# Moving three waits of a split-precision decoder trunk: gate statistics, the first convolution, and the first head's scores, transposes and values

## The chip, the cores and the metric

The kernel runs on one core of a Trainium2 chip. The metric is device time of one execution in microseconds (us), the median of the runs shown; all arithmetic is in the kernel, and the weights come from HBM in every execution. The engines are called as the profile calls them: PE is TensorE (PEld its weight loads), DVE is VectorE, ACT is ScalarE, POOL is GpSimd and SP is SyncE, which here issues the DMAs.

## The reference

A decoder trunk of two layers over 256 tokens with 1024 channels, in float32. Layer 0 mixes tokens by a gated short convolution, layer 1 by dilated window attention with 8 heads of 128 and three groups per head, each group with its own q, k, v and its own dilation. After each mixer come a squared-ReLU MLP (1024 to 4096 and back) and a gated per-layer input. In short:

```python
def rmsnorm(x, g):
    y = xf * lax.rsqrt(jnp.mean(xf * xf, axis=-1, keepdims=True) + RMS_EPS)
    return y * g
...
h = h + mixed
h = h + squared_relu_mlp(rmsnorm(h, norm_mlp[i]), mlp_w_up[i], mlp_w_down[i])
ple_gate = jax.nn.sigmoid(rmsnorm(h, norm_ple[i]) @ ple_w_gate[i])
h = h + ple_gate * (p[i] @ ple_w_proj[i])
```

Attention of a head: for each of the three groups scores of q and k under that group's mask, softmax, and the groups joined by their log-sum-exp. The kernel does this as one softmax over the 512 masked scores of the three groups, which is the same.

## The kernel before, in words

**Split products.** Every float32 matrix product is made of three products of rounded parts. A weight slab of up to 8 blocks of 128x128 is loaded by SP (L321), ACT rounds it to a high part `whi` (L331) and DVE subtracts to get the low part `wlo` (L280, in `sub`). There are 6 buffers for split slabs, and a slab is asked for up to 5 slabs ahead (L337). Activations are split likewise into pairs (`split_into`, L402 on ACT and L280 on DVE; `h_ready`, L411 on ACT and L412 on DVE). A block (L342) is 3 matmuls of kind "n" or "t", or 2 of kind "w", all at L363.

**The plan.** `make_plan` writes the order of the work as one list: blocks, and between them steps ("do", name, ...). `tile_trunk` emits the instructions in that order, and the build then sets a fixed order of instructions on each engine, which may differ a little from the list: an instruction whose operands its own estimate has ready later can come behind some that follow it in the list. At run time each engine takes its instructions strictly in its order.

**The convolution (layer 0).** For each pair of channel tiles c come the products C, X and B. `stat(0)` (L441) makes the norm's statistics: matmuls with ones (L445), a power on POOL (L435), two small corrections on DVE, and a diagonal matrix of the result, split in two parts (L477, L478). `spread(0)` (L480) multiplies the diagonals with ones on PE (L486), and ACT copies the row out of PSUM (L488). `conv(0)` (L548) needs that row; it has one memset of 0.1 us on POOL (L551). Both stand behind block k = 1 of C of the second pair.

**The gate of layer 0 (`gate_plan`).** Four products `gate(j)` of 16 blocks each, j being a pair of channel tiles. `gate_out(j)` (L590) multiplies by the spread row on DVE (L592), takes the sigmoid on ACT (L593), multiplies and adds on DVE (L594, L600) and makes by `h_ready` the pair x3_j that layer 1 multiplies, and the sums of squares for its norm. The first product of attention, head 0's q and k, takes x3_0 to x3_3 in order, three groups side by side.

**Attention.** Head 0's q and k of all three groups (kind "n") come first, with `stat(3)` and `spread(3)`, which scales the tables `cosr` and `sinr` of the rotation (L491, L492) on DVE. Then for each group `qk_out` (L604) rotates q and k on POOL: one multiply by cosr (L606), two by sinr (L609) and an add (L615). Group 0 is then split (L402 on ACT, L280 on DVE). A later head h runs 16 blocks of q and k per group (kind "w"), `add_up` (L382 on ACT, L383 on DVE) and `qk_out` after each group, then v (16 blocks, "t", `v_out`). The head before is worked off in between: `scores(h-1)` (L632; matmuls of group 0 at L638, of groups 1 and 2 at L641; mask and maximum on DVE at L644; exponential and scaling on ACT at L648 and L650) behind group 0 of head h, `turn(h-1)` (L653, eight transposes at L659) behind group 2, and `values(h-1)` (L667; L674, L680, out of PSUM at L691 and L692) behind block k = 5 of v. None of the three issues a DMA or a POOL instruction. PSUM has 8 banks from one pool; each accumulator or score tile takes one. Plain activation tiles (`act`) have 13 buffers, pairs 20.

Of the kernel before, what the change touches and what calls it, by code (L numbers as in the profile page):

```python
# [18 lines left out]
NK = D // P  # L19
# [46 lines left out]
def mlp_plan(layer):  # L66
    up, down, x = f"up{layer}", f"down{layer}", f"x{3 * layer + 1}"
    plan = head_start(up, "u", x, ("up_out",))
    for j in range(2, FF // P // 2):
        for k in range(NK):  # L70
            for i in (0, 1):
                plan.append(("w", up, k, 2 * j + i, ("u", j), i, x))
        plan.append(("do", "up_out", j))
        if j == 3:
            plan.append(("do", "stat_rows", 3 * layer + 1))
        if (layer, j) == (0, 8):
            plan.append(("do", "rope"))
    for j in range(NP):
        for k in range(FF // P):
            for i in (0, 1):  # L80
                plan.append(("n" if j == NP - 1 else "w", down, k, 2 * j + i, ("d", j), i, "u"))
        plan.append(("do", "down_out", layer, j))
    return plan


def proj_plan():
    plan = []
    for j in range(NP):
        for k in range(PLE // P):
            for i in (0, 1):  # L90
                plan.append(("n", "proj0", k, 2 * j + i, ("p", j), i, "p0"))
        plan.append(("do", "proj_out", j))
    return plan


def gate_plan():
    def gate(j, ks):
        return [("n", "gate0", k, 2 * j + i, ("g", j), i, "x2") for k in ks for i in (0, 1)]

    plan = gate(0, range(6)) + gate(1, range(6)) + gate(0, (6, 7)) + [("do", "stat", 2)]  # L100
    plan += gate(1, (6, 7)) + gate(2, range(5)) + [("do", "spread", 2)]
    plan += [("do", "gate_out", 0), ("do", "gate_out", 1)] + gate(2, range(5, NK)) + [("do", "gate_out", 2)]
    return plan + gate(3, range(NK)) + [("do", "gate_out", 3)]


def last_plan():

    plan = []

    def gate(ks, b, c):  # L110
        return [("t", "gate1", k, c, ("g", b, c), b, "x5") for k in ks]

    for k in range(NK - 3):
        for b in (0, 1):
            plan += gate((k,), b, 0) + gate((k,), b, 1)
        if k == 3:
            plan.append(("do", "stat", 5))
        if k:
            plan.append(("do", "turn_h", k - 1))
    for b in (0, 1):  # L120
        for c in (0, 1):
            plan += gate(range(NK - 3, NK), b, c)
            plan.append(("do", "last_gate", b, c))
            if b and c:
                plan.append(("do", "last_scale", 0, 0))
            cuts = 2 if b and c else 1
            for m in range(cuts):
                for k in range(PLE // P):
                    plan.append(("t", "proj1", k, c, ("p", b, c, m), b, "p1", m, cuts))
                plan.append(("do", "last_out", b, c, m, cuts))  # L130
        plan.append(("do", "last_rms", b))
    return plan + [("do", "last_scale", 1, 0), ("do", "last_scale", 1, 1)]


def make_plan():
    plan = [("do", "begin")]
    plan += proj_plan()
    for c in range(NP):
        for s, what in ((1, "C"), (2, "X"), (0, "B")):
            for k in range(NK):  # L140
                for i in (0, 1):
                    kind = "w" if what == "X" else "n"
                    plan.append((kind, "sc_in", k, s * NK + 2 * c + i, (what, c), i, "x0"))
                if c == 0 and (what, k) in ((("C", 3), ("C", 7), ("X", 1), ("X", 3))):
                    plan.append(("do", "squares", 0, (3, 7, 1, 3).index(k) if what == "C" else 2 + (k == 3)))
                if (c, what, k) == (0, "B", 2):
                    plan.append(("do", "stat", 0))
                if (c, what, k) == (1, "C", 1):
                    plan += [("do", "spread", 0), ("do", "conv", 0)]
            if what == "X":  # L150
                plan.append(("do", "add_up", (what, c)))
        if c:
            plan.append(("do", "conv", c))

    def mix(key, j, ks):
        return [("n", key, k, 2 * j + i, ("o", j), i, "y") for k in ks for i in (0, 1)]

    for k in range(6):
        plan += mix("sc_out", 0, (k,)) + mix("sc_out", 1, (k,))
    for j in range(NP):  # L160
        plan += mix("sc_out", j, range(6 if j < 2 else 0, NK)) + [("do", "mix_out", 0, j)]
    plan += mlp_plan(0) + gate_plan()

    plan.append(("do", "masks"))

    def qk(h, g, ks):
        return [
            ("w" if h else "n", "qkv", k, (i, g, h), ("qk", h, g), i, "x3") for k in ks for i in (0, 1)
        ]

    def v(h, ks):
        return [("t", "v", k, h, ("v", b, h), b, "x3") for k in ks for b in (0, 1)]

    for kp in range(NP):
        if kp == NP - 1:
            plan.append(("do", "stat", 3))
        for g in range(GROUPS):
            plan += qk(0, g, (2 * kp, 2 * kp + 1))
    plan += [("do", "add_up", ("qk", 0, g)) for g in range(GROUPS)]
    plan += v(0, (0, 1)) + [("do", "spread", 3)]  # L180
    plan += [("do", "qk_out", 0, g) for g in range(GROUPS)] + v(0, range(2, NK)) + [("do", "v_out", 0)]

    def sums(h, g):
        return [("do", "add_up", ("qk", h, g)), ("do", "qk_out", h, g)]

    for h in range(1, HEADS):
        plan += qk(h, 0, range(NK)) + sums(h, 0) + [("do", "scores", h - 1)]
        plan += qk(h, 1, range(NK)) + sums(h, 1)
        plan += qk(h, 2, range(NK)) + [("do", "turn", h - 1)] + sums(h, 2)
        plan += v(h, range(6)) + [("do", "values", h - 1)] + v(h, range(6, NK)) + [("do", "v_out", h)]  # L190

    last = HEADS - 1
    plan += [x for k in (0, 1, 2) for j in range(NP) for x in mix("w_o", j, (k,))]
    plan.append(("do", "scores", last))
    plan += [x for k in (3, 4) for j in range(NP) for x in mix("w_o", j, (k,))]
    plan.append(("do", "turn", last))
    plan += [x for k in (5, 6) for j in range(NP) for x in mix("w_o", j, (k,))]
    plan.append(("do", "values", last))
    for j in range(NP):
        plan += mix("w_o", j, (7,)) + [("do", "mix_out", 1, j)]  # L200
    plan += mlp_plan(1) + [("do", "last_load")] + last_plan()
    return plan
# [658 lines left out]
```

## Time and profile before

| | us |
|---|---|
| median of 3 runs (lowest, highest) | 806.48 (806.38, 806.66) |
| the profiled execution, its own time | 803.92 |
| its span, from the first to the last instruction | 802.1 |
| PE busy in that span | 779.4 |
| DVE, ACT, POOL busy | 584.2, 443.1, 180.9 |

The profile is of one execution. Times in its rows are counted from the start of the span. Busy time of PE counts a matmul from its start to its modelled end, so neighbouring matmuls overlap. An idle time is put down to the event that ended it.

### The profile page before, as it was taken

To read this page: it belongs to the slowest core of one execution; us is meant where nothing else is said; L and a number is where in the kernel's file an instruction comes from. 1 tells how busy PE (TensorE), PEld (TensorE's weight loads), DVE (VectorE), ACT (ScalarE), POOL (GpSimd) and SP (SyncE) were. 2 spreads that over 40 slices of the span, in tenths; PEclk is the share of its full clock that TensorE was granted. 3 is DMA by queue.
4 is the path that set the end of the run, shared out by engine and by line. 5 is a ranking of instruction groups with operands and counts; after the bars stand their busy time and mean duration, and the time that the engine had idled before them with its cause. 6 is when DMAs were issued, how large, how long until landed. Compare 5 with 4: busy or idle time off the path is not lost.

```text
span 802.1 us, 12773 instructions
## 1 busy us (share of the span) xinstructions
PE 779.4 (97%) x4986; PEld 713.9 (89%) x4986; DVE 584.2 (73%) x818; ACT 443.1 (55%) x672; POOL 180.9 (23%) x117
## 2 busy tenths in 40 slices
PE   8999999999999999959999999999999999999996
PEld 8999998888888999949999899999988888888985
DVE  6987778898456658857697798788599787555555
ACT  8655565666444446636556656647566565444453
POOL 0100000000000000197487687687000000000001
PEclk9999999999999999979999999999999999999998
DMA  8865555555555554534464465465546555565521
GB/s 288 291 211 190 181 187 177 192 179 189 184 186 187 183 185 154 171 93 142 125 204 148 145 194 154 149 186 172 178 152 201 189 186 190 188 198 185 185 79 54
DMA packets 41676, 140.98 MB, mean 176 GB/s; under 512 B 4752, under 2 KB 5136, under 8 KB 41616
## 3 DMA queue, kind: packets, MB, share of 16 engines
q1 hardware_dynamic: 41616, 140.17, 54.8%
q8 instruction: 39, 0.64, 0.3%
q14 instruction: 21, 0.17, 0.1%
HBM read 139.10 MB, written 1.05 MB: 175 GB/s over the span
## 4 chain that ended last, share of the span: by engine, by line
PE 91%; DVE 3%; POOL 3%; issue 1%; ACT 1%; DMA 1%; SPq 0%; POOLq 0%; DVEq 0%; ACTq 0%
PE acc_d L363 22%; PE acc_u L363 22%; PE acc_qk L363 15%; PE acc_v L363 7%; PE acc_o L363 6%; PE acc_g L363 5%; PE acc_X L363 3%; PE acc_B L363 2%; PE acc_C L363 2%; POOL rot L609 1%; DVE wlo L280 1%; PE sc L641 1%; PE o L680 1%; PE tp L659 1%; PE o L674 1%
## 5 line engine op out<-in xcount | busy, mean ns | idle before, releaser
L280 DVE TENSOR_TENSOR wlo<-raw,whi 128x1024 fp32r<-128x1024 f32 (+3 forms) x273 | 367.2, 1353 | 133.5 <-ACT whi L331 132.8
L331 ACT ACTIVATE whi<-raw 128x1024 fp32r<-128x1024 f32 (+3 forms) x273 | 276.9, 1017 | 198.2 <-PE acc_d L363 87.3
L363 PE MATMUL acc_d<-u,whi 128*128 128x512 f32 (+1 forms) x640 | 180.6, 350 | 0.0
L363 PE MATMUL acc_u<-x,whi 128*128 128x512 f32 x512 | 179.4, 395 | 0.0
L363 PE MATMUL acc_d<-u,wlo 128*128 128x256 f32 x512 | 143.9, 281 | 0.0
L363 PE MATMUL acc_u<-x,wlo 128*128 128x256 f32 x512 | 143.4, 280 | 0.0
L363 PE MATMUL acc_qk<-x,whi 128*128 128x512 f32 (+1 forms) x432 | 135.6, 371 | 1.9 <-DVE x L412 1.9
L363 PEld LDWEIGHTS acc_d<-u,whi 128*128 128x128 f32 x640 | 111.9, 189 | 16.9
L435 POOL TENSOR_TENSOR n<-v,power 128x4 f32<-128x4 f32 (+1 forms) x6 | 6.5, 1087 | 518.7 <-DVE v L455 515.9
L363 PEld LDWEIGHTS acc_u<-x,whi 128*128 128x128 f32 x512 | 95.9, 187 | 22.4
L363 PE MATMUL acc_qk<-x,wlo 128*128 128x256 f32 x384 | 107.9, 283 | 0.5 <-ACT x L411 0.3
L363 PEld LDWEIGHTS acc_d<-u,wlo 128*128 128x128 f32 x512 | 97.1, 190 | 0.0
L363 PEld LDWEIGHTS acc_u<-x,wlo 128*128 128x128 f32 x512 | 96.7, 189 | 0.0
L363 PEld LDWEIGHTS acc_qk<-x,whi 128*128 128x128 f32 x432 | 78.1, 190 | 16.2 <-DVE x L412 2.5
L609 POOL TENSOR_TENSOR rot<-qk,sinr 16x512 f32<-16x512 f32 x48 | 90.6, 1887 | 3.3
L363 PEld LDWEIGHTS acc_qk<-x,wlo 128*128 128x128 f32 x384 | 72.8, 191 | 0.9 <-ACT x L411 0.9
L363 PE MATMUL acc_v<-whi,x 128*128 128x384 f32 x256 | 68.8, 339 | 0.0
L606 POOL TENSOR_TENSOR qk<-qk,cosr 128x512 f32<-128x512 f32 x24 | 36.9, 1539 | 54.4 <-DVE qk L383 47.7
L363 PEld LDWEIGHTS acc_v<-whi,x 128*128 128x128 f32 x256 | 46.5, 188 | 0.0
L363 PE MATMUL acc_o<-y,whi 128*128 128x256 f32 x256 | 46.0, 283 | 0.0
L615 POOL TENSOR_TENSOR qk<-qk,rot 48x512 f32<-48x512 f32 x24 | 43.9, 1828 | 1.7
L363 PE MATMUL acc_v<-wlo,x 128*128 128x384 f32 x128 | 42.8, 335 | 0.0
(164 smaller groups left out, 1036.3 us busy)
## 6 DMA issues: line engine op xcount, KB each, us to landing
raw<-in_w SPq DMA_DIRECT2D x232, 512.0 KB, 3.6
raw<-in_w SPq DMA_DIRECT2D x32, 384.0 KB, 3.1
raw<-in_w SPq DMA_DIRECT2D x7, 256.0 KB, 4.7
h<-in_xT SPq DMA_DIRECT2D x4, 256.0 KB, 5.0
out<-ht SPq DMA_DIRECT2D x4, 256.0 KB, 2.0
pt<-in_pT SPq DMA_DIRECT2D x2, 256.0 KB, 3.6
mask<-in_mask SPq DMA_DIRECT2D x2, 256.0 KB, 4.3
gain<-in_gain SPq DMA_DIRECT2D x2, 256.0 KB, 4.5
```

Source lines behind the costliest of these rows:

```text
L280: nc.vector.tensor_tensor(out, a, f32(b), ALU.subtract)
L331: nc.scalar.activation(hi[:, :width], t[:, :width], AF.Copy)
L363: nc.tensor.matmul(to, a, b, start=n == 0 and name not in opened, stop=n == len(products) - 1 and left[name, half if kind == "n" else 0] == 0,
L435: nc.gpsimd.tensor_tensor(y, v, power[:, : v.shape[1]], ALU.pow)
L606: nc.gpsimd.tensor_tensor(t, p, both(cosr), ALU.mult)
L609: nc.gpsimd.tensor_tensor(r[dst : dst + 16], p[src : src + 16], sinr[src : src + 16].unsqueeze(1).to_broadcast([16, 2, S]), ALU.mult,)
L615: nc.gpsimd.tensor_tensor(t[:48], t[:48], r[:48], ALU.add)
L641: nc.tensor.matmul(ps[:, (g + 1) * P : (g + 2) * P], t[:, 0, own], t[:, 1, own], start=True, stop=True)
L659: nc.tensor.transpose(ps[n // 2][:, n % 2, b * P : (b + 1) * P], sm[:, n * P : (n + 1) * P], ident)
L674: nc.tensor.matmul(ps[:, 0, :], a, b[:, kb, :], start=kb == 0 and n == 0, stop=False, skip_group_check=True)
L680: nc.tensor.matmul(ps[:, 0, b * P : (b + 1) * P], v12[:, b, g * P : (g + 1) * P], t[:, g, b * P : (b + 1) * P], start=False, stop=g == 1, ...
```

## The change

It touches only the order of the plan. In the gate, `stat(2)` comes behind 16 blocks, `spread(2)` behind 28 and `gate_out(0)` with it; they came behind 28 and 42. The order of the gate's blocks among themselves stays. In the convolution, `spread(0)` and `conv(0)` come behind block k = 4 of C instead of k = 1. In attention, the first head alone is worked off later: `scores(0)` behind group 2 of head 1 instead of group 0, `turn(0)` behind block k = 5 of head 1's v, and `values(0)` behind group 0 of head 2. Later heads keep their order.

```diff
-    plan = gate(0, range(6)) + gate(1, range(6)) + gate(0, (6, 7)) + [("do", "stat", 2)]
-    plan += gate(1, (6, 7)) + gate(2, range(5)) + [("do", "spread", 2)]
-    plan += [("do", "gate_out", 0), ("do", "gate_out", 1)] + gate(2, range(5, NK)) + [("do", "gate_out", 2)]
-    return plan + gate(3, range(NK)) + [("do", "gate_out", 3)]
+    plan = gate(0, range(6)) + gate(1, (0, 1)) + [("do", "stat", 2)] + gate(1, range(2, 6)) + gate(0, (6, 7))
+    plan += [("do", "spread", 2), ("do", "gate_out", 0)] + gate(1, (6, 7)) + [("do", "gate_out", 1)]
+    return plan + [x for j in (2, 3) for x in (*gate(j, range(NK)), ("do", "gate_out", j))]
...
-                if (c, what, k) == (1, "C", 1):
+                if (c, what, k) == (1, "C", 4):
                     plan += [("do", "spread", 0), ("do", "conv", 0)]
...
     for h in range(1, HEADS):
-        plan += qk(h, 0, range(NK)) + sums(h, 0) + [("do", "scores", h - 1)]
-        plan += qk(h, 1, range(NK)) + sums(h, 1)
-        plan += qk(h, 2, range(NK)) + [("do", "turn", h - 1)] + sums(h, 2)
-        plan += v(h, range(6)) + [("do", "values", h - 1)] + v(h, range(6, NK)) + [("do", "v_out", h)]
+
+        late, steps = h == 1, [[("do", what, h - 1)] for what in ("scores", "turn", "values")]
+        plan += qk(h, 0, range(NK)) + ([("do", "values", 0)] if h == 2 else []) + sums(h, 0)
+        plan += [] if late else steps[0]
+        plan += qk(h, 1, range(NK)) + sums(h, 1) + qk(h, 2, range(NK)) + steps[late ^ 1] + sums(h, 2)
+        plan += v(h, range(6)) + steps[2 - late] + v(h, range(6, NK)) + [("do", "v_out", h)]
```

## Rows read from the trace of the kernel before

**Rows 1.** The page, busy time of each engine, share of the span, instructions.

```profile
PE 779.4 (97%) x4986; PEld 713.9 (89%) x4986; DVE 584.2 (73%) x818; ACT 443.1 (55%) x672; POOL 180.9 (23%) x117
```

**Rows 2.** Waits of PE, whole span: us in total, times, longest.

```profile
PE sc L641 <- POOL qk L615: 7.9, 2, 4.8
PE acc_qk L363 <- DVE x L412: 1.9, 3, 0.6
...
PE spread L486 <- DVE diag L477: 0.7, 1, 0.7
```

**Rows 3.** Windows: head 0's q and k, head 1, head 2; length, then busy per engine.

```profile
341.80:383.44 41.64, 32.84 (x183) 29.61 (x183) 25.98 (x31) 19.18 (x33) 35.70 (x23) 0.88 0.41 122
383.44:412.51 29.07, 29.07 (x183) 27.01 (x182) 21.28 (x29) 17.20 (x30) 18.26 (x11) 1.00 0.48 151
...
311.91:333.24 21.33, 19.00 (x151) 17.98 (x150) 18.84 (x39) 12.74 (x20) 1.01 (x1) 1.00 0.56 175
```

**Rows 4.** The chain that ended last, in order of time: start, length, what.

```profile
83.76 23.04 PE acc_o L363 x192
...
360.27 12.37 PE acc_qk L363 x64
...
379.76 0.71 PE o L674 x6
...
381.36 2.08 PE acc_v L363 x12
383.44 5.55 PE acc_qk L363 x32
...
390.60 11.11 PE acc_qk L363 x64
```

**Rows 5.** Timeline of DVE around the gate: start, length, what, idle before.

```profile
305.53 0.68 DVE L592 TENSOR_TENSOR gs<-acc_g,row 128x512 f32<-128x512 f32 x1
...
310.77 0.89 DVE L412 SCALAR_TENSOR_TENSOR x<-hr,gains,x 128x256 fp32r<-128x256 f32 x2 [0.85 <-ACT x L411]
...
328.21 0.87 DVE L412 SCALAR_TENSOR_TENSOR x<-hr,gains,x 128x256 fp32r<-128x256 f32 x2
```

**Rows 6.** Timeline of POOL, rotations of heads 0 and 1.

```profile
338.37 1.34 POOL L606 TENSOR_TENSOR qk<-qk,cosr 128x512 f32<-128x512 f32 x1 [6.48 <-DVE cosr L491]
...
356.67 1.25 POOL L615 TENSOR_TENSOR qk<-qk,rot 48x512 f32<-48x512 f32 x1
...
362.53 1.28 POOL L615 TENSOR_TENSOR qk<-qk,rot 48x512 f32<-48x512 f32 x1
...
382.21 2.16 POOL L615 TENSOR_TENSOR qk<-qk,rot 48x512 f32<-48x512 f32 x1
```

**Rows 7.** Tile qk on POOL: duration ns min/median/max, first and last start.

```profile
L609 POOL TENSOR_TENSOR rot<-qk,sinr x48: 1252/1896/2184, 339.8 to 558.1; 16x512 f32<-16x512 f32 x48
L606 POOL TENSOR_TENSOR qk<-qk,cosr x24: 1267/1297/2191, 338.4 to 553.7; 128x512 f32<-128x512 f32 x24
L615 POOL TENSOR_TENSOR qk<-qk,rot x24: 1252/2154/2285, 345.5 to 560.4; 48x512 f32<-48x512 f32 x24
```

**Rows 8.** Timeline of ACT, splits of group 0 and first softmax.

```profile
346.81 0.63 ACT L402 ACTIVATE qk<-qk 128x512 fp32r<-128x512 f32 x1 [5.78 <-POOL qk L615]
...
361.41 0.72 ACT L648 ACTIVATE sm<-sm,st 128x512 f32<-128x512 f32 x1 [8.29 <-DVE st L647]
...
363.85 0.63 ACT L402 ACTIVATE qk<-qk 128x512 fp32r<-128x512 f32 x1 [1.62 <-POOL qk L615]
...
366.44 0.71 ACT L650 ACTIVATE sm<-sm,st 128x512 f32<-128x512 f32 x1
```

**Rows 9.** The page's group of DVE's weight splits: busy, mean ns, idle before.

```profile
L280 DVE TENSOR_TENSOR wlo<-raw,whi 128x1024 fp32r<-128x1024 f32 (+3 forms) x273 | 367.2, 1353 | 133.5 <-ACT whi L331 132.8
```

**Rows 10.** Windows of 1 us: length, busy PE, PEld, DVE, ACT, POOL, then granted clock.

```profile
352.00:353.00 1.00, 0.00 (x0) 0.00 (x0) 1.00 (x2) 1.00 (x1) 1.00 (x2) 0.83 0.97 266
...
362.00:363.00 1.00, 1.00 (x5) 0.90 (x4) 0.32 (x2) 0.23 (x2) 0.92 (x2) 0.55 0.87 135
```

## The prediction

> **What bounds the kernel now.** I first read the busy times: PE is busy 97% of the span [rows 1], so only two things can be won, a hole in PE or a stretch at a lower clock; every matmul stays. Next I read what PE waited for [rows 2]. Three waits stand there that the change is near: 7.9 us in the first head's scores for POOL's rotation, 1.9 us in head 0's q and k for the gate's x3 pairs, 0.7 us for the diagonal of the convolution's statistics. A wait shows only time in which PE had nothing at all in flight, so I priced each hole by windows instead [rows 3]. Head 1 takes 41.64 us, head 2 takes 29.07, with the same instructions: 12.57 us are lost there, more than the wait says. Part of that is clock: it fell between 352 and 353 us, with PE idle in that window, to the lower level of 1.2 GHz (a mean of 0.83 in that microsecond), and came back only between 362 and 363 (a mean of 0.55) [rows 10], though PE ran on again from 358. So some 4.9 us of work ran at half speed, 2.4 us lost. Head 0's q and k take 21.33 us for 144 matmuls; at 0.12 us each (192 in 23.04 [rows 4]) and 0.37 for the statistics between them they need 17.65, so 3.7 us are lost.
>
> All times below are on the axis of the trace of before; what an earlier part wins shifts the later ones as a whole.
>
> **The gate.** Nothing is added: the order of the weights stays, so no DMA is moved; the only POOL instruction of these steps is one power, with POOL idle around it. A block is 3 x 0.12 = 0.36 us, so the statistics come 12 blocks or 4.3 us earlier and the spread 14 blocks or 5.0 us. gate_out(0) began on DVE at 305.53 [rows 5]; its own accumulators are complete at the new spread, so it can begin at about 300.5. The pair x3_0 was complete at 311.66, x3_3 at 329.08, one each 5.8 us [rows 5]. Shifted by 5.0 and at the same pace they come at 306.6, 312.5, 318.3 and 324.1; PE wants them at 311.9 and then each 12 blocks or 4.3 us later, the last at 324.9. So nothing waits any more, with 0.8 us to spare at the last. The new cover of statistics to spread is 12 blocks, 4.3 us. If DVE puts a split (1.35 us [rows 9]) into that chain, PE waits a little at the spread and the last pair is late by 0.5. Bounds: 3.7 gained, or 1.9 if only the wait shown goes and the rest stays. I take 3.6, as DVE has holes before 310 that the earlier chain fills.
>
> **The convolution.** The spread moves by 3 x 2 x 3 = 18 matmuls or 2.2 us, and the wait was 0.7 [rows 2]: 0.7 gained. conv(0) gives its PSUM banks back up to 1.5 us later; five banks are held then and the next product takes two, so two are left. Bounds: 0.7 gained, or 0.5 lost if the banks were short. I take 0.7.
>
> **The first head.** No instruction is added. Three things decide, in this order.
>
> First, scores(0). Now PE reaches it at 347.35, while head 0's last rotation ends at 357.92 [rows 6]. Moved behind two more groups (11.11 us [rows 4]) it is reached at 358.5. That wait is gone, up to 1 us.
>
> Second, POOL. It starts at 338.37 and is the same as before: six rotations have to be done before scores(1) can end. A rotation is two sinr products, one cosr product and an add: by the smallest durations 5.0 us, by the medians 7.24, by the largest 8.84 [rows 7]. Six of them end at 368.5, 381.8 or 391.4. Without any wait scores(1) would end at 390.60 - 12.57 = 378.03; some 0.8 us of it follow the last rotation. So by POOL alone the part gains 12.6, 8.0, or it loses 1.6. The spread of these durations goes with DVE's splits: the adds at 356.67 and 362.53, with DVE idle, took 1.25 and 1.28 us, the one at 382.21, beside splits, 2.16 [rows 6].
>
> By the Trainium skill, SBUF — State Buffer, section "Who interferes with whom", a DVE instruction with two SBUF inputs and a GpSimd instruction that reads SBUF lock each other out, and the one that issues second blocks entirely. That speaks against this change, since DVE's splits now go on where they stood still; what it would make of the time stands with the last rival.
>
> Third, ACT. Its split of group 0 (L402) waits for POOL, and all behind it waits too: 5.78 us for head 0, 1.62 for head 1 [rows 8]. In the order of before, head 1's L402 stands between the exponential at 361.41 and the last scaling at 366.44 [rows 8], within 2 us of scores in the build's estimate, which thus takes a rotation to be much quicker than it is. With scores(0) moved away, I expect L402 of head 1 ahead of the sums of its groups 1 and 2, of three or four weight splits and of the softmax of head 0. POOL ends that rotation at 357.92 plus a rotation beside an idle DVE, 5.0, so at about 363 (362.53 + 1.28 = 363.81 before [rows 6]); I take 363.3. PE has slabs until about 364: at 352 the splits reach to block k = 3 of head 1's v. From 363.3: L402 0.63; then DVE, the slower of the two, has four splits of 1.35 (5.4) and two sums at some 0.65 each (the nearest row is L402's 0.63) before the mask of scores(0): 370.6. From the first exponential to the end of the last scaling went 367.15 - 361.41 = 5.74 us, of which 1.62 + 0.63 were L402, now done before: 3.5, so the softmax is ready at 374.1. Eight transposes (0.96 by 0.12 each) end at 375.1, where PE would have been at 367. Then blocks 6 and 7 of v 2.08, q and k 5.55, values 1.60 (379.76 to 381.36) and scores 1.61 (388.99 to 390.60) [rows 4]: scores(1) ends at 385.9, by when POOL, restarted at about 366.5, has its two rotations done (381 to 384). Gained: 390.60 - 385.9 = 4.7. PE's wait of some 7 us would again cost clock, between 0 and the 2.4 lost before; half of v's first transposes break it, and I take 1.1. So 3.6 us for this part, between 2.3 and 4.7 if ACT blocks, and up to 8.0 if it does not.
>
> values(0) comes behind group 0 of head 2. Its output is wanted only by w_o much later; it holds two activation tiles longer, by my count 11 of 13. Costs nothing; were the pool short, v_out(1) would wait and keep two PSUM banks, under 1 us.
>
> **Sum.** 3.6 + 0.7 + 3.6 = 7.9 us of the profiled execution's 803.92, so 796.0 there. The median of the runs is 806.48, 0.3% more; 806.48 - 7.9 = 798.6, and I say 798.5.
>
> **Rivals.** POOL alone is the limit. ACT's L402 stands further back than I think, or the splits catch up quicker: 3.6 + 0.7 + 8.0 = 12.3, so 794.2. For it: the medians of 24 rotations; against it: the order in ACT's queue.
>
> All of the hole goes: 3.6 + 0.7 + 12.57 = 16.9, so 789.6. It needs six rotations by about 377, at 6.4 us each. For it: head 0's three took 19.55 together [rows 6], 6.5 each; against it: that was partly with DVE idle behind scores, and head 1's last ended at 384.37.
>
> The gate does not gain, or the change does not do there what it says: the build sets the order by its own estimate and may put the statistics back behind other blocks, or DVE, busy 18.84 of 21.33 us in head 0's q and k [rows 3], stays the limit. Then 4.3, so 802.2.
>
> Slower: POOL is locked out by the splits that now never pause. If each of the four instructions of a rotation waited out a whole split of 1.35, a rotation would take 5.0 + 5.4 = 10.4, six end at 400.9 and scores(1) at 401.7, 11.1 later than before; less the 4.3 of the other parts that is 6.8 slower, 813.3. It becomes slower than before by more than can be measured once head 1's last rotation ends after 395.7 (390.60 - 0.8 + 4.3 + 1.6). For it: an add takes 1.25 alone and 2.15 mostly; against it: the largest durations make 8.84, not 10.4, and only some ten splits fall into the stretch, 13.5 us in all, so that 30.1 + 13.5 puts the six where the medians do. The rule of the Trainium skill named above taken at its word gives this price; the trace agrees that one waits for the other, not that each does every time.
>
> **Numbers.** About 0.2% (1.6 us) can be told from no change. Chances: forecast 0.47 (its own range 795.5 to 801), POOL alone 0.27, all of the hole 0.10, gate without gain 0.11, slower 0.05. The range from 792 to 803 holds the first, second and fourth. Faster 0.92: all but the slower case and some of the fourth; same 0.04, slower 0.04.
>
> **What would show it.** Right: no wait of PE for x3 pairs and at spread(0), head 0's q and k in 17.7 to 18.5 us; no wait at scores(0); a long wait of ACT at head 1's L402 with splits queued behind, PE waiting at v's block 4 or the transposes for up to 8 us, and head 1 shorter while head 2 is no shorter than 29 us. POOL alone: PE waits at L641 of scores(1) for 4 to 5 us instead, none at the transposes. Wrong: PE waits in the gate's spread, or for a PSUM bank in the second X.

## The result, and the profile after

The changed kernel takes 800.23 us, the median of 6 runs (798.31 to 802.65), against 806.1 for the kernel before (6 runs, 803.4 to 806.66). The ratio is 0.9936, 95% interval 0.9909 to 0.9963: 3 to 7 us faster, 5.9 by the medians. The forecast was 798.5, between 792 and 803. The runs of either kernel lie in two groups (before at 803.4 to 803.5 and 805.8 to 806.7, after at 798.3 to 799.1 and 801.3 to 802.7), and the median after falls between its two; group by group the gain is about 4.5 to 4.8 us.

The profiled executions differ by less, 803.92 and 801.64, mostly because PE took 3.0 us longer in the changed kernel's for the MLP of layer 1, in which no step was moved; that comes at the end. So I read stage by stage, each from its own start. Busy time first, of the changed kernel's page:

```profile
span 799.9 us, 12768 instructions
PE 780.3 (98%) x4986; PEld 713.9 (89%) x4986; DVE 583.1 (73%) x818; ACT 442.6 (55%) x672; POOL 179.0 (22%) x117
```

The work is the same as in [rows 1]. What changed is PE's list of waits (us in total, times, longest), against [rows 2]:

```profile
PE tp L660 <- ACT sm L651: 8.7, 1, 8.7
...
PE sc L642 <- POOL qk L616: 0.2, 1, 0.2
```

The waits for x3 pairs and for the convolution's diagonal have gone from the list, and 0.2 us are left at the scores. One of 8.7 us has come: the first head's transposes wait for its softmax. (Lines of the changed kernel are one higher than before.)

**The convolution.** From the first C to the start of the mixer's output product (`acc_o`) the chain of before has 83.76 - 15.92 = 67.84 us and that of after 83.28 - 16.34 = 66.94: 0.90 gained. The start itself was 0.42 later: the first weight load in the chain took 5.39 us, 4.56 before. First the start in the chain of before, then both points in the chain of after:

```profile
15.92 3.14 PE acc_C L363 x24
```

```profile
16.34 3.13 PE acc_C L364 x24
...
83.28 23.04 PE acc_o L364 x192
```

**The gate.** Timelines of PE and DVE in the changed kernel, and the window of head 0's q and k (length, then busy time of PE):

```profile
293.48 0.51 PE L446 MATMUL ssq<-ones,tot 128*128 128x2 f32 x4
298.24 0.40 PE L487 MATMUL spread<-diag,ones_r 128*128 128x256 f32 x2
...
324.65 0.61 PE L446 MATMUL ssq<-ones,tot 128*128 128x2 f32 x4
```

```profile
299.28 0.69 DVE L593 TENSOR_TENSOR gs<-acc_g,row 128x512 f32<-128x512 f32 x1
...
322.92 0.89 DVE L413 SCALAR_TENSOR_TENSOR x<-hr,gains,x 128x256 fp32r<-128x256 f32 x2
```

```profile
311.43:329.52 18.09, 17.99 (x151) 17.78 (x149) 16.64 (x35) 10.78 (x17) 1.01 (x1) 1.00 0.60 197
```

The first gate_out begins at 299.28 instead of 305.53 [rows 5], and the last pair is complete at 323.81 instead of 329.08. The window has 18.09 us instead of 21.33 [rows 3]: 3.24 gained. Against 17.65 of pure work 0.44 are left, most of it at the statistics of the next norm (L446 at 324.65): they stand ahead of the last pair's blocks, and the sums of squares they need were complete on DVE only at 324.59.

**The first head.** From the first matmul of head 1 to the end of scores(1), in windows of before and of after:

```profile
341.80:390.60 48.80, 40.00 (x229) 36.07 (x229) 30.38 (x40) 23.54 (x41) 37.27 (x24) 0.90 0.44 132
```

```profile
338.08:385.33 47.25, 38.32 (x229) 35.03 (x229) 30.58 (x39) 22.88 (x41) 35.39 (x23) 0.93 0.46 134
```

The same 229 matmuls, and only 1.55 us gained of the 12.57 that were lost. Even that is no steady figure: over three profiles of each kernel (two more of each stand under "Two paces of PE") the stretch has 48.21 us before and 47.81 after on the mean, 0.40 gained, and the two overlap. ACT's timeline in the changed kernel shows the reason, in its order:

```profile
347.25 1.60 ACT L332 ACTIVATE whi<-raw 128x768 fp32r<-128x768 f32 x2
360.93 0.63 ACT L403 ACTIVATE qk<-qk 128x512 fp32r<-128x512 f32 x1 [12.09 <-POOL qk L616]
361.47 0.64 ACT L383 ACTIVATE qk<-acc_qk 128x256 f32<-128x256 f32 x2
362.00 1.79 ACT L332 ACTIVATE whi<-raw 128x768 fp32r<-128x768 f32 x2
363.68 0.66 ACT L383 ACTIVATE qk<-acc_qk 128x256 f32<-128x256 f32 x2
364.20 1.07 ACT L332 ACTIVATE whi<-raw 128x1024 fp32r<-128x1024 f32 x1
...
369.66 0.72 ACT L649 ACTIVATE sm<-sm,st 128x512 f32<-128x512 f32 x1 [3.08 <-DVE st L648]
...
371.17 1.32 ACT L651 ACTIVATE sm<-sm,st 128x512 f32<-128x512 f32 x2
```

For 12.09 us ACT stands at the split of head 1's group 0 (L403), which waits for POOL. Behind it in the queue are two pairs of sums, three weight splits and then the softmax. DVE, whose half of the split waits for ACT's, stands too:

```profile
361.60 0.69 DVE L281 TENSOR_TENSOR qk<-qk,qk 128x512 fp32r<-128x512 f32 x1 [8.48 <-ACT qk L403]
```

PE had split weights up to block 5 of v and did not starve, but then, in its own timeline:

```profile
371.93 1.97 PE L660 MATMUL tp<-ident,sm 128*128 128x128 f32 x8 [8.72 <-ACT sm L651]
```

The idle time cost clock as well. In the changed kernel's windows of 1 us the granted clock falls between 368 and 369 us, with PE idle, to the lower level (0.50 from 369 to 375); it is back between 375 and 376, when PE had run again for 3 us. So the eight transposes took 1.97 us instead of 0.87 in other heads.

```profile
368.00:369.00 1.00, 0.00 (x0) 0.00 (x0) 1.00 (x1) 0.00 (x0) 0.92 (x2) 0.60 0.75 303
...
375.00:376.00 1.00, 1.00 (x7) 1.00 (x6) 1.00 (x2) 1.00 (x2) 1.00 (x1) 0.98 0.00 0
```

Sum to the end of scores(1) in this pair of profiles: 0.90 + 3.24 + 1.55 = 5.7 us. On the mean of the three profiles of each kernel, with the convolution taken from PE's first matmul of C, it is 0.75 + 3.25 + 0.40 = 4.4 us, close to the gain group by group; the first pair flatters the change.

### The profile page after: what moved, and what is told of

Same layout as the page of the kernel before. It is cut to its first block, busy times and chain, and to the rows that moved or that the text cites. A ratio compares the mean times of both kernels' runs of the same rounds, so it can differ in the third digit from the quotient of the medians.

```text
span 799.9 us, 12768 instructions
## 1 busy us (share of the span) xinstructions
PE 780.3 (98%) x4986; PEld 713.9 (89%) x4986; DVE 583.1 (73%) x818; ACT 442.6 (55%) x672; POOL 179.0 (22%) x117
## 4 chain that ended last, share of the span: by engine, by line
PE 89%; POOL 3%; DVE 3%; ACT 1%; issue 1%; DMA 1%; SPq 0%; POOLq 0%; DVEq 0%; ACTq 0%
PE acc_d L364 23%; PE acc_u L364 23%; PE acc_qk L364 13%; PE acc_v L364 7%; PE acc_o L364 6%; PE acc_g L364 5%; PE acc_B L364 3%; PE acc_X L364 3%; PE acc_C L364 3%; POOL rot L610 2%; DVE wlo L281 1%; PE tp L660 1%; PE o L681 1%; PE sc L642 1%; POOL qk L616 1%
## 5 line engine op out<-in xcount | busy, mean ns | idle before, releaser
L364 PEld LDWEIGHTS acc_d<-u,whi 128*128 128x128 f32 x640 | 112.1, 190 | 18.1
L610 POOL TENSOR_TENSOR rot<-qk,sinr 16x512 f32<-16x512 f32 x48 | 88.2, 1838 | 3.3
```

The lines of the kernel that those rows point to most:

```text
L364: nc.tensor.matmul(to, a, b, start=n == 0 and name not in opened, stop=n == len(products) - 1 and left[name, half if kind == "n" else 0] == 0,
L610: nc.gpsimd.tensor_tensor(r[dst : dst + 16], p[src : src + 16], sinr[src : src + 16].unsqueeze(1).to_broadcast([16, 2, S]), ALU.mult,)
```

## The experiments

**The parts alone.** In the first the heads' loop is that of before; in the second the gate and the convolution are.

```diff
-        plan += [] if late else steps[0]
-        plan += qk(h, 1, range(NK)) + sums(h, 1) + qk(h, 2, range(NK)) + steps[late ^ 1] + sums(h, 2)
...
+        plan += qk(h, 0, range(NK)) + sums(h, 0) + [("do", "scores", h - 1)]
```

> Only the gate's statistics and the first convolution's spread are moved; the heads keep the order of before. Theory (nearly all of the gain is these two, the head part is eaten by ScalarE's wait at head 1's split of group 0): about 4.1 us less than before, 802.0; head 0's q and k without a wait; head 1 takes 41.6 us as before with PE's wait of 8 us at L641. Rival (the head part brings most of the gain): at most 2 us less than before, 804 or more.

Measured: 802.31 (6 runs; before 806.66 in 17 runs), ratio 0.9942, 0.9923 to 0.996, 4.4 us less by the medians. Head 1 to the end of scores(1), 337.46 to 385.68, has 48.22 us, within the 47.9 to 48.8 of the kernel before, and PE's wait is the old one:

```profile
PE sc L640 <- POOL qk L614: 7.9, 2, 4.8
```

> Only the first head's scores, transposes and values are moved. Theory: 1.0 to 2.0 us less than before, 804.5; from the start of head 1's q and k to the end of scores of head 1 about 47.3 us instead of 48.8, with PE's wait of some 8 to 9 us at the transposes and ScalarE's of some 12 us at the split. Rival (the head part brings most): 4 us less or more, 802 or under.

Measured: 804.69 (12 runs), ratio 0.9973, 0.996 to 0.9986: 2.0 us less by the medians. The stretch from 342.02 to 389.40 has 47.38 us, as expected, though the changed kernel's three profiles range from 47.25 to 48.37; and the waits are those of the changed kernel, PE's a little shorter (7.6 us against 8.7). PE's and ACT's, in the kernel with the heads alone:

```profile
PE tp L661 <- ACT sm L652: 7.6, 1, 7.6
```

```profile
ACT qk L404 <- POOL qk L617: 36.1, 8, 12.1
```

The gate and the convolution bring most of the gain, the heads little, as the theory had it; the two add up to the whole within the intervals.

**Taking the split out of the way.** The changed kernel, but head 1's split of group 0 is a step of its own behind turn(0):

```diff
-        if g == 0:
-            split_into("qk", head, t)
+        if g == 0 and head != 1:
+            split_qk(head)
...
-        plan += v(h, range(6)) + steps[2 - late] + v(h, range(6, NK)) + [("do", "v_out", h)]
+        plan += v(h, range(6)) + steps[2 - late] + ([("do", "split_qk", 1)] if late else [])
+        plan += v(h, range(6, NK)) + [("do", "v_out", h)]
```

> The changed kernel, and the split of head 1's group 0 on ScalarE and VectorE stands behind the first head's transposes instead of behind its rotation. Theory (ScalarE's in-order wait for GpSimd holds back splits, sums and softmax): ScalarE's wait of 12 us goes, PE's wait at the transposes falls from 8.7 us to under 1, and scores of head 1 end 38 to 41 us after the start of head 1's q and k instead of 47.3, held by the sixth rotation: about 793.5. Rival (GpSimd's rotations are what all waits for, the queue of ScalarE does not matter): the scores of head 1 still end at 46 us or later, and the time is within 1.5 us of the changed kernel's, 799 to 801.

Measured: 797.43 (4 runs), ratio 0.988, 0.9861 to 0.99. In this kernel ACT splits head 1's group 0 without any wait, and PE waits no more at the transposes; it now waits for POOL, 0.8 us at scores(0) and 4.8 at scores(1):

```profile
366.40 0.63 ACT L404 ACTIVATE qk<-qk 128x512 fp32r<-128x512 f32 x1
```

```profile
PE sc L646 <- POOL qk L617: 5.6, 2, 4.8
```

```profile
380.28 0.80 PE L646 MATMUL sc<-qk 128*128 128x128 f32 x2 [4.83 <-POOL qk L617]
```

So the split in ACT's queue, with DVE's half of it, was what held the changed kernel; that is shown. (The two halves were moved together, so what either does alone is not.) How much it gives was expected too high: the stretch of head 1 to the end of scores(1) is 382.57 - 339.00 = 43.6 us, 3.7 to 4.8 less than in the changed kernel's three profiles, neither the 38 to 41 of the theory nor the 46 of the rival. POOL's last rotation of head 1 ends later than I took it to. First and last instruction of the six in this kernel:

```profile
335.57 1.34 POOL L608 TENSOR_TENSOR qk<-qk,cosr 128x512 f32<-128x512 f32 x1 [7.96 <-DVE cosr L493]
...
378.36 1.86 POOL L617 TENSOR_TENSOR qk<-qk,rot 48x512 f32<-48x512 f32 x1
```

They take 44.65 us, 7.44 each, where the medians of [rows 7] gave 7.24. And the wait cost clock again, behind scores(1): the granted clock was 0.50 from 379 to 385 us, and the next 64 matmuls took 12.62 us where they took 11.11 in the kernel before [rows 4]. So of some 4 us won 1.5 were lost again.

```profile
382.57 12.62 PE acc_qk L365 x64
```

**Is it POOL then?** The same kernel with one product of head 0's rotation on DVE:

```diff
-        nc.gpsimd.tensor_tensor(t, p, both(cosr), ALU.mult)
+        engine = nc.vector if head == 0 and g == 2 else nc.gpsimd
+        engine.tensor_tensor(t, p, both(cosr), ALU.mult)
```

> The kernel with the late split, and the cosr product of the first head's group 2 runs on VectorE instead of GpSimd. Theory (in that kernel the sixth rotation on GpSimd is what scores of head 1 wait for): GpSimd ends the six about 1.3 to 2.2 us earlier, PE's wait at L641 of 5.6 us falls to 3 to 4.3 us. Rival (the wait is set by when the sums of head 1's groups 1 and 2 arrive, or by VectorE, which has the product more to do now): the wait stays at 5 us or more.

Measured, a single run: 797.05. PE's wait for POOL, where it stands, and POOL's first and last instruction of the six:

```profile
PE sc L647 <- POOL qk L618: 4.2, 1, 4.2
```

```profile
376.99 0.80 PE L647 MATMUL sc<-qk 128*128 128x128 f32 x2 [4.23 <-POOL qk L618]
```

```profile
333.91 1.34 POOL L609 TENSOR_TENSOR qk<-qk,cosr 128x512 f32<-128x512 f32 x1 [7.96 <-DVE cosr L493]
...
375.08 1.85 POOL L618 TENSOR_TENSOR qk<-qk,rot 48x512 f32<-48x512 f32 x1
```

PE waits 1.4 us less in all, as the theory has it: the 0.8 at scores(0) are gone, and at scores(1), which PE reaches sooner, it is 4.2 instead of 4.8. Plainer is the end: POOL's six now take 43.0 us instead of 44.65, and scores(1) ends 379.27 - 337.35 = 41.9 us after head 1's start instead of 43.6, so both come 1.6 us earlier together. The sixth rotation on POOL is what the kernel with the late split waits for. (The single time says little: this run has the longer pace of the last experiment, the profile without the move the shorter.)

**Giving POOL time.** If POOL lags once, by head 0's three rotations at a stroke, and has some 7 us to spare in every head (29.07 less three rotations of 7.24), all heads can be worked off as late as the first, and it catches up behind PE:

```diff
+        plan += qk(h, 0, range(NK)) + ([("do", "values", h - 2)] if h > 1 else []) + sums(h, 0)
+        plan += qk(h, 1, range(NK)) + sums(h, 1) + qk(h, 2, range(NK)) + [("do", "scores", h - 1)] + sums(h, 2)
+        plan += v(h, range(6)) + [("do", "turn", h - 1)] + ([("do", "split_qk", h)] if h < HEADS - 1 else [])
+        plan += v(h, range(6, NK)) + [("do", "v_out", h)]
...
+    plan += [x for j in range(NP) for x in mix("w_o", j, (0,))] + [("do", "values", last - 1)]
...
+        if g == 0 and head in (0, HEADS - 1):
+            split_qk(head)
```

> The changed kernel with all heads but the last worked off as late as the first, and with the late split for heads 1 to 6. Theory: GpSimd catches up over several heads behind PE, no wait of PE over 0.5 us is left between head 0 and the last; head 1's stretch takes about 29 us like the others: 11 us less than the changed kernel, about 789. Rival (GpSimd is too slow for this pace, some 22 to 26 us of rotation in each head of 29 us): waits for GpSimd of 3 us or more come back at the scores of head 2 or 3, and the time is no better than that of the kernel with the late split alone.

Measured: 790.7 (4 runs), ratio 0.9807, 0.9789 to 0.9825: 16 us less than before, 9.5 less than the changed kernel by the medians, and the best version here. Windows of its heads 1 and 2, each from the first matmul of group 0 to that of the next head (length, busy PE, PEld, DVE, ACT, POOL, clock):

```profile
338.64:367.33 28.69, 27.87 (x169) 25.55 (x169) 21.46 (x27) 18.12 (x31) 27.83 (x17) 1.00 0.46 151
367.33:396.44 29.11, 29.11 (x183) 27.06 (x182) 25.08 (x30) 16.48 (x30) 28.25 (x17) 1.00 0.50 164
```

Head 1 is as short as any other, at full clock, while POOL is busy for 28 of 29 us in both: it is catching up, and PE hardly waits (0.8 us once at the first scores, for POOL, and 0.8 us once at the values of head 6, for DVE, a little over the 0.5 expected). The 14 matmuls that its window has fewer are those of values, which now come in the next head's.

**Is the late order enough by itself?** The same without the late split:

```diff
-        plan += v(h, range(6)) + [("do", "turn", h - 1)] + ([("do", "split_qk", h)] if h < HEADS - 1 else [])
+        plan += v(h, range(6)) + [("do", "turn", h - 1)]
...
-        if g == 0 and head in (0, HEADS - 1):
+        if g == 0:
             split_qk(head)
```

> All heads but the last worked off late, but each split of group 0 stays behind its rotation. Theory (the late split is what frees ScalarE): head 1 shows the same waits as the changed kernel, ScalarE some 12 us at the split and PE 8 to 9 us at the transposes, and the time is 8 to 11 us above that of the kernel with all heads late and the late split: 799 to 802. Rival (working all heads off late is enough, since scores of head 1 come 10 us later too): PE waits under 3 us at the transposes and the time is at most 794.

Measured, a single run: 805.86. PE's and ACT's waits in this kernel:

```profile
PE tp L662 <- ACT sm L653: 8.7, 1, 8.7
PE o L677 <- DVE pT L280: 2.6, 1, 2.6
```

```profile
ACT qk L402 <- POOL qk L615: 50.8, 8, 12.1
```

Head 1 is that of the changed kernel again, so the late split is needed. The time is 4 us above what I expected. Against the profiled execution of the kernel with all heads late and the late split (790.89) it is 15.0 us: 10.2 up to the end of scores(1), within the 8 to 11 expected; 3.0 in the later heads, 2.6 of them the new wait at the values of head 6; and 2.6 by the longer pace of the next point, less 0.85 by an earlier start.

**Two paces of PE.** The changed kernel twice more, and the kernel before twice more, unaltered.

> The changed kernel once more, unaltered. Theory (one program has two paces of PE in the MLP of layer 1, 66.6 and 89.6 us or 67.8 and 90.9 us for the same 384 and 576 matmuls, and these make most of the spread of 2 to 4 us among its runs): either 801.5 with the long stretches, as its first profile had, or about 799 with the short ones; all stages before are as in the first profile within 0.5 us. Rival (the pace belongs to the built program, by where its tiles lie): the long stretches again, whatever the time is.

> The changed kernel a third time, for the same question as the run before it: both paces of PE in layer 1's MLP in profiles of one program, or always the long one.

> The kernel of before once more, unaltered. Its first profile had the short stretches in layer 1's MLP (66.6 and 89.6 us) and a time of 803.92, 2.6 us under the median of the runs. Theory (one program has both paces): long stretches (67.8 and 90.9 us) with a time of about 806.5, all else as in the first profile. Rival (the pace belongs to the built program): short stretches again, whatever the time is.

> The kernel of before a third time, for the same question: the long stretches with about 806.5, or the short ones with about 804 again.

Measured: 801.81 and 802.28 for the changed kernel, 804.01 and 803.25 for the kernel before. The MLP of layer 1 in the chains of one profile each, the changed kernel's first:

```profile
603.76 67.84 PE acc_u L364 x384
671.61 90.87 PE acc_d L364 x576
```

```profile
608.55 66.56 PE acc_u L363 x384
675.11 89.58 PE acc_d L363 x576
```

All three profiles of the changed kernel have the long stretches, all three of the kernel before the short ones, and that speaks for the rival, that the pace belongs to the built program. But it does not hold for the 128 matmuls of the MLP ahead of these: in the kernel before they took 22.29 us in the first profile and 22.67 in both later ones. The chain of the first, then of the second:

```profile
585.93 22.29 PE acc_u L363 x128
```

```profile
585.64 22.67 PE acc_u L363 x128
```

There one program did run at both paces. So neither my theory nor the rival is shown.

I had also expected all earlier stages within 0.5 us of the first profile. Head 0's q and k are (21.3 us before, 18.1 after in all), but head 1 to the end of scores(1) is not. The two further profiles of the kernel before, then the two of the changed kernel:

```profile
342.29:390.27 47.98, 39.16 (x229) 35.36 (x229) 29.61 (x40) 23.54 (x41) 37.13 (x24) 0.89 0.42 136
```

```profile
341.69:389.55 47.86, 39.05 (x229) 35.23 (x229) 30.11 (x40) 23.53 (x41) 37.13 (x24) 0.89 0.41 135
```

```profile
337.13:385.50 48.37, 39.43 (x229) 36.16 (x229) 30.56 (x39) 22.98 (x41) 35.36 (x23) 0.89 0.41 137
```

```profile
338.17:385.98 47.81, 38.87 (x229) 35.58 (x229) 30.57 (x39) 22.98 (x41) 35.37 (x23) 0.89 0.41 136
```

PE's waits are the same each time (8.7 us at the transposes after, 7.9 to 8.0 at the scores before). What differs is how much work PE did at the lower clock behind them: the 12 matmuls of v behind the transposes took 2.68, 3.79 and 3.23 us in the three profiles of the changed kernel (2.08 in a later head), and the 64 of q and k behind scores(0) 12.37, 11.53 and 11.43 in those of the kernel before (11.11 in a later head).

## Why the prediction was right, and where it was off

The time lies in the range and the sign is right. The likeliest case was the right one: that ACT's in-order wait at head 1's split eats most of the hole that the head part was to close. Point by point, by the steps of the prediction:

- **The gate**, 3.6: 3.24. The first pair came 6.2 us earlier, the last 5.3, of which 0.5 is the convolution's (0.90 less the later start); 5.0 was taken. The 0.4 missing are mostly the statistics behind the last pair, which I had not put into the chain; 0.8 us to spare at the last pair were not enough for them.
- **The convolution**, 0.7: 0.90, or 0.75 on the mean of the three profiles of each kernel. PE's list shows no wait for a PSUM bank.
- **scores(0)** without a wait, up to 1 us: 0.2. Right.
- **The transposes**: a wait of about 7 us was expected, with the split ahead of two sums, three or four splits and the softmax. That order is what ACT's timeline shows (three splits), and the wait was 8.7.
- **The size of the head part**, 3.6 with 2.3 to 4.7 if ACT blocks: 1.55 in the first pair of profiles and 0.40 on the mean of three, below the range either way; this is the term that was mis-sized. In the first pair two steps of it failed. The release of the split was put at 363.3, 21.5 us after head 1's start; it came at 360.93 - 338.08 = 22.9. I had head 0's last rotation end as before, but two v splits, which before stood behind the mask of scores(0), now ran beside it: its two sinr products took 3.86 us where they took 2.56 before, and DVE's two splits beside them 3.35, as POOL's timeline and DVE's in the changed kernel show.

```profile
350.40 3.86 POOL L610 TENSOR_TENSOR rot<-qk,sinr 16x512 f32<-16x512 f32 x2
```

```profile
349.76 3.35 DVE L281 TENSOR_TENSOR wlo<-raw,whi 128x768 fp32r<-128x768 f32 x2
```

  And the softmax was put 10.8 us after the release; the last scaling ended 372.49 - 360.93 = 11.6 after it, as a split of 2.32 us stood between the maximum and its negative on DVE. Together these are 2.1 us. The low clock cost 1.1 in the transposes and 0.6 in the next 12 matmuls of v, 0.6 more than the 1.1 that I had taken; and the transposes began 0.6 us before the last scaling ended, which I had not counted on. The two cancel, and 2.1 is what is missing from 3.6. What is missing beyond that on the mean is clock, by the matmuls named under "Two paces of PE": 1.2 us lost in the 12 of v on the mean where the first profile had 0.6, and 0.7 in the 64 of q and k before where the first had 1.3.
- **The rivals.** POOL alone: false for this kernel, true for the one with the late split, where PE waits at scores(1) (L646) for 4.8 us as that case said, though its stretch gains 4.3 to 5.2 and not 8.0. All of the hole: not in this order, but with all heads late it closes. The gate without gain: false. Slower, by POOL being locked out: false. In the kernel with the late split, where DVE pauses only twice for more than a microsecond, the six rotations took 7.44 us each, not 10.4: POOL lost 14.5 us in 24 instructions against the smallest durations, some 0.6 each and not a whole split of 1.35. That is near the 13.5 that I had held against this case. By the Trainium skill (SBUF — State Buffer, "Who interferes with whom") the one of the two that issues second is blocked until the other has ended. The rows agree that both get longer (two splits, of 0.96 us each alone, took 3.35 beside POOL), and not that every POOL instruction waits for a whole split.

Of the whole, 7.9 was expected; 5.9 came by the medians, 5.7 by the stages of the first pair, and 4.4 by those of all three. That the median lies so near the forecast is in part luck: with a gain of 4.4 to 4.8 us it would be 801.3 to 801.7, still in the range, but outside the 795.5 to 801 that I had given the forecast case itself.

## What to carry to other kernels

When a step is moved away from a wait, look at what stands between on the engines that do not wait yet: an in-order queue that holds a dependent of the slow engine (here ACT's split behind POOL's rotation) will take the wait over as soon as the bound engine runs on, and everything behind it comes late together. Move the dependent with the step; here that was worth more than the move itself (some 4 us in that stretch, 1.5 of which the clock took back, against 0.40). And where a slow engine lags only once, all later consumers can be shifted by the same lag, here at the price of two waits of 0.8 us, while shifting the first alone brought the wait back one step on.

## What the hardware showed that was not expected

The same instructions of PE run at two paces at full granted clock: 384 matmuls in 66.56 or 67.84 us and 576 in 89.58 or 90.87, 2.6 us together, with no wait in between. In layer 0 all profiles have the long ones. In layer 1 the kernel before, the one with the late split and the one with all heads late with that split have the short ones, all others the long ones, so the profiles of before and after lie 2.6 us nearer together than the moved steps make them, 3.0 with the 128 matmuls ahead of these. Those 128 changed pace between profiles of one program. What decides the pace is open. It is also open whether the spread among executions without a profile comes from it, since only those with a profile show it.
